# Four block products of seven multiplications per feed-forward input instead of three, and a pitch of 272 for the activations' halves

## The chip, the cores and the metric

The kernel runs on one core of a Trainium2 chip. The metric is the device time of one execution in microseconds (us). The kernel before was run three times: 2631.84, 2633.85 and 2634.01 us, median 2633.85 us. Engines are named as the profile names them: PE is the matrix engine (its weight loads are listed apart, as PEld), DVE the vector engine, ACT the scalar engine, POOL the GpSimd engine, SP the engine that issues most transfers.

## What is computed

A trunk of two layers over 256 tokens of 2048 features, all in float32. Each layer has three sublayers, and each ends in a residual sum and a layer norm:

```python
x <- LN(a*x + 0.5*SwiGLU_1(x))
x <- LN(a*x + Mixer_i(x))        # layer 0: attention, layer 1: causal pooling
x <- LN(a*x + 0.5*SwiGLU_2(x))

def swiglu(x, w_in, w_out):
    a, gate = jnp.split(x @ w_in, 2, axis=-1)
    return (jax.nn.silu(a) * gate) @ w_out
```

So there are four feed-forward blocks. In each, `w_in` is 2048 x 8192: 4096 columns for `a` and 4096 for `gate`. They are taken as eight column pairs, a pair being 512 columns of `a` and the 512 of `gate` that they are multiplied with. `w_out` is 4096 x 2048.

## The kernel before, in words

**Precision.** A float32 product is made of fp32r matmuls. Every operand is split in two: ACT rounds it into a high half (a cast to fp32r), and DVE subtracts that from the source and leaves the low half. A product is high x high + high x low + low x high, accumulated in PSUM. Activations are kept split, weights are split as they arrive. The activations of the trunk are `xs` (line 60): four tiles of 128 partitions x 4 x 2 x `W`, with `W` = 258: 256 tokens and two columns that carry the gain and the bias of the norm ahead (written by `Norm.__init__`, line 224). `xs[k][:, 0]` is the high half of block k, `xs[k][:, 1]` the low one, 258 floats (1032 bytes) further on.

**The input side of a feed-forward block** is `ffn_in`, called four times. It makes the eight column pairs in three ways:

- Pair 0 by `gemm`, feature by feature, where the norm ahead is applied meanwhile.
- Pairs 1 to 4 in plain columns: `column` (line 327) takes 128 columns of `w_in` over all 2048 rows as one transfer of 1 MB into a `raw` tile, splits it in two halves of 128 x 1024 (ACT line 324, DVE line 325), and runs for each of the 16 blocks of rows one matmul of 512 columns (line 341) and one of 256 (line 345). ACT copies the bank out (line 350), DVE adds its two halves (line 524). Two such columns, one of `a` and one of `gate`, make a feature, so a pair is eight units of this kind: every second unit ends in a silu on ACT (line 529), the others in a product on DVE (line 535). There are 32 units in each `ffn_in`.
- Pairs 5 to 7 (`SEVENS` = 3) by `Seven.run` (line 377): tokens, rows and columns are halved, and seven products of half-size blocks take the place of eight (Strassen-Winograd). For each of eight steps i it loads 1 MB of weights, splits two of the blocks as they are (512 and 1024 elements a partition), forms `ta` (1024) and `tb` (twice 512) on DVE (line 400), splits these too (1024 each), and runs seven products of three matmuls of 512 columns (lines 422 to 424). Seven PSUM banks are held by it; the eighth is for units. At its end ACT copies one bank and DVE makes seven sums of 512 (line 434), then come silu on ACT and two products of 512 on DVE (line 473), and, later, sixteen transposes of 128 columns on PE (line 481), two to a copy of ACT (line 483 has four copies). The stationary operands of its first products are `xs`; the others are `s` tiles that `Seven.prepare` makes once per `ffn_in`.

**The order around the change.** Units are emitted into the block products by `between`, a function that `Seven.run` calls after each half of a step: in the version before, after the second half of steps 0 to 6 and the first half of step 7, so eight per pair, and one more when the pair is done. Four units stand ahead of the first pair, one behind the last. After the last pair come `settle` (line 107 on ACT, line 108 on DVE: the split of the 32 gated features, as `g`) and the product with `w_out` (lines 164, 167; its weights are split at lines 140 and 141). The emitted order is the priority of each instruction; a planner that simulates the program fixes the order on each engine before the run, and moves units, settles and first splits of `w_out` where it sees an engine free. At run time each engine works in that order.

**Buffers.** Three `raw` tiles, six `whi` and six `wlo` tiles of 128 x 1024. A unit takes two of each, a step of `Seven.run` three and a half. The DVE and ACT work on weights can therefore be less than two steps ahead of PE.

**Memory.** `vecs` (line 96) holds 176 floats. The tiles of the activations, the weights and the features lie behind it. In pooling, `evac_u` (line 693) takes its `u` from a pair of buffers of its own, tag `z`.

Of the kernel before, what the change touches and what calls it, by code (L numbers as in the profile page):

```python
# [8 lines left out]
F32 = mybir.dt.float32  # L9
F32R = mybir.dt.float32r  # L10
# [3 lines left out]
P = 128  # L14
T = 256
D = 2048
KT = D // P
W = T + 2
WARM = 9
FF = 2 * D  # L20
HEADS = 8
INNER = HEADS * P
WINDOWS = (2, 4, 8, 16)

SEVENS = 3
PARTS = ('', '_columns', '_seven')
ALPHA = 4 ** 0.25
SB_SCALE = P ** -0.5
# [2 lines left out]
VECS = [  # L31
    'l0_ln1_g', 'l0_ln1_b', 'l0_ln2_g', 'l0_ln2_b', 'l0_ln3_g', 'l0_ln3_b',
    'l1_ln1_g', 'l1_ln1_b', 'l1_ln2_g', 'l1_ln2_b',
    'l1_pool_scale',
]
# [3 lines left out]
def trunk(ctx: ExitStack, tc: tile.TileContext, a: dict, out: bass.AP):  # L39
    nc = tc.nc  # L40
    const = ctx.enter_context(tc.tile_pool(name="const", bufs=1))
# [15 lines left out]
    xq = [res.tile([P, 4, T], F32, tag=f"xq{q}", name=f"xq{q}") for q in range(4)]  # L57
    xf = [x[:, j] for x in xq for j in range(4)]

    xsq = [res.tile([P, 4, 2, W], F32R, tag=f"xs{q}", name=f"xs{q}") for q in range(4)]  # L60
    xs = [x[:, j] for x in xsq for j in range(4)]
    whole = [x[:, :, :T] for x in xs]

# [29 lines left out]
                   allow_small_or_imprecise_dtypes=True)  # L93
    rcount = const.tile([P, WINDOWS[-1]], F32, name="rcount")
    nc.vector.reciprocal(rcount, count)
    vecs = const.tile([P, len(VECS) * KT], F32, name="vecs")

    def vec(name, t):
        c = VECS.index(name) * KT + t
# [113 lines left out]
    class Norm:  # L213
# [3 lines left out]
        def __init__(self, gname, bname):  # L217
            self.g, self.b = gname, bname
            self.sums = res.tile([P, 2, 2 * T], F32, tag="sums", name="sums")
            lo, hi = VECS.index(gname) * KT, VECS.index(bname) * KT  # L220
            gb = vecs[:, lo:lo + 2 * KT].rearrange("p (j t) -> p t j", j=2)
            assert hi == lo + KT
            for q in range(4):
                h, l = (xsq[q][:, :, i, T:] for i in range(2))
                nc.scalar.copy(h, gb[:, 4 * q:4 * q + 4])
                nc.vector.tensor_tensor(out=l, in0=gb[:, 4 * q:4 * q + 4], in1=h.bitcast(F32), op=ALU.subtract)

# [219 lines left out]
    def ffn_in(w_in, w_columns, w_seven, norm, hooks=None):  # L447
# [108 lines left out]
        lates = []  # L556

        def between(i, h):
            if h == 1 or i == 7:
                unit()  # L560
            if lates and (i, h) == (0, 1):
                lates.pop()()
# [121 lines left out]
    def pooling(p, norm):  # L684
# [5 lines left out]
        def evac_u(grp, nm):  # L690
            def evac(f, ps):
                win = WINDOWS[grp]
                u = tmp.tile([P, T], F32, tag="z", name="u")
                bias = total(u, ps, nm)
                if bias is not None:
                    nc.scalar.activation(u, u, AF.Identity, bias=bias)
                s, n = u, 1
                while n < win:
                    s2 = tmp.tile([P, T], F32, tag="win", name="win")
                    nc.vector.tensor_copy(s2[:, :n], s[:, :n])  # L700
                    nc.vector.tensor_tensor(out=s2[:, n:], in0=s[:, n:], in1=s[:, :T - n], op=ALU.add)
                    s, n = s2, 2 * n
                q = wide("q")[:, :T]
                nc.vector.tensor_tensor(out=q[:, :win], in0=s[:, :win], in1=rcount[:, :win], op=ALU.mult)
                nc.vector.tensor_scalar(out=q[:, win:], in0=s[:, win:], scalar1=1.0 / win, scalar2=None, op0=ALU.mult)
                nc.vector.tensor_tensor(out=q, in0=q, in1=u, op=ALU.subtract)
                split(pooled[4 * grp + f], q, q)
            return evac
# [35 lines left out]
    def last(p, norm):  # L744
        w_out = a[f'{p}ffn2_w_out']
        c = 0.5 / ALPHA
        z = [None] * 4
# [12 lines left out]

        gs = ffn_in(*(a[f'{p}ffn2_w_in' + x] for x in PARTS), norm, hooks=turn)
        for i, name in enumerate((f'{p}ln3_g', f'{p}ln3_b')):
            gb = res.tile([P, 4, 2 * W], F32, tag=f"xs{i}", name=f"gb{i}")
            for q in range(4):
                gq = gb[:, q, :512]
                nc.gpsimd.dma_start(gq, a[name][q * 512:(q + 1) * 512].partition_broadcast(P))
                gains.append(gq)
# [101 lines left out]
```

## Time and profile before

| what | value |
|---|---|
| median of three runs | 2633.85 us |
| the profiled execution, its own time | 2632.2 us |
| its span, first to last instruction | 2630.5 us |
| PE busy | 2612.0 us, 99% |
| PEld busy | 2277.8 us, 87% |
| DVE busy | 2084.0 us, 79% |
| ACT busy | 1518.1 us, 58% |
| POOL busy | 11.9 us |
| moved by DMA | 499.53 MB, mean 190 GB/s |
[...]

Busy time is the time in which an engine has at least one instruction running. Instructions of one engine overlap at their ends, so the duration of one is longer than the distance from its start to the next start; what an engine can do in a stretch is read from the starts. Matmul ends are modelled, so PE at 99% may still be slower than it could be.

### The profile page before, as it was taken

How to read it: one execution, taken by the hardware profiler on the slowest of the kernel's cores; microseconds unless marked ns; L12 is line 12 of the kernel's file. 1: busy time of each engine (PE TensorE's matmuls, PEld its weight loads, DVE VectorE, ACT ScalarE, POOL GpSimd, SP SyncE). 2: the span in 40 equal slices, each digit the busy share in tenths (PEclk: the TensorE clock that was granted, in tenths of full speed). 3: DMA queues.
4: the chain of work that ended last, by engine and by line, in shares of the span. 5: the costliest groups of instructions: out<-in, count | busy, mean ns of one | idle time of the engine just before them, and what ended most of it. 6: DMA issues, size and time to landing. Idle time of an engine off the chain costs nothing.

```text
span 2630.5 us, 37467 instructions
## 1 busy us (share of the span) xinstructions
PE 2612.0 (99%) x14828; PEld 2277.8 (87%) x14828; DVE 2084.0 (79%) x2798; ACT 1518.1 (58%) x2130; POOL 11.9 (0%) x28
## 2 busy tenths in 40 slices
PE   9999999999999999999999999999999999999998
PEld 8888888899997888888988888889888898888886
DVE  7899967585689989765799897657878799999645
ACT  6565654466576656644666566445555566656432
POOL 0000000000000000000000000000000000000000
PEclk9999999999999999999999999999999999999999
DMA  7555555554455555555455555554555545555653
GB/s 262 187 208 178 206 209 184 187 179 161 156 177 176 202 198 202 199 180 195 171 191 192 192 196 207 190 192 162 203 183 190 188 154 195 200 198 202 230 195 119
DMA packets 71519, 499.53 MB, mean 190 GB/s; under 512 B 7984, under 2 KB 8624, under 8 KB 12080
## 3 DMA queue, kind: packets, MB, share of 16 engines
q1 hardware_dynamic: 70704, 495.05, 53.7%
q8 instruction: 116, 1.90, 0.3%
q0 software_dynamic: 640, 2.10, 0.2%
q14 instruction: 59, 0.48, 0.1%
HBM read 495.02 MB, written 2.10 MB: 189 GB/s over the span
## 4 chain that ended last, share of the span: by engine, by line
PE 94%; DVE 3%; ACT 1%; issue 1%; DMA 0%; SPq 0%; DVEq 0%; ACTq 0%
PE ps L164 21%; PE pc L341 17%; PE ps L167 11%; PE pc L345 9%; PE p L422 5%; PE p L423 5%; PE p L424 5%; PE ps L159 4%; PE ps L158 4%; PE ps L160 4%; PE y L806 2%; PE y L804 2%; PE y L805 2%; DVE wlo L325 1%; PE v L660 1%
## 5 line engine op out<-in xcount | busy, mean ns | idle before, releaser
L141 DVE TENSOR_TENSOR wlo<-raw,whi 128x1024 fp32r<-128x1024 f32 (+1 forms) x498 | 595.9, 1200 | 407.7 <-ACT whi L140 407.2
L140 ACT CAST whi<-raw 128x1024 fp32r<-128x1024 f32 (+1 forms) x498 | 510.1, 1032 | 548.3 <-PE ps L164 336.6
L341 PE MATMUL pc<-xs,whi 128*128 128x512 f32 x2048 | 729.2, 396 | 1.4 <-ACT gw L483 0.7
L345 PE MATMUL pc<-xs,wlo 128*128 128x256 f32 x2048 | 554.9, 281 | 0.0
L164 PE MATMUL ps<-g,whi 128*128 128x512 f32 x1536 | 537.7, 396 | 0.0
L325 DVE TENSOR_TENSOR wlo<-raw,whi 128x1024 fp32r<-128x1024 f32 (+1 forms) x448 | 487.9, 1103 | 39.3 <-ACT whi L324 21.6
L324 ACT CAST whi<-raw 128x1024 fp32r<-128x1024 f32 (+1 forms) x448 | 417.7, 959 | 164.0 <-PE pc L341 110.8
L341 PEld LDWEIGHTS pc<-xs,whi 128*128 128x128 f32 x2048 | 385.1, 189 | 87.3 <-ACT gw L483 2.6
L167 PE MATMUL ps<-g,wlo 128*128 128x256 f32 x1536 | 427.3, 280 | 0.0
L345 PEld LDWEIGHTS pc<-xs,wlo 128*128 128x128 f32 x2048 | 386.7, 189 | 11.4
L164 PEld LDWEIGHTS ps<-g,whi 128*128 128x128 f32 x1536 | 287.1, 188 | 66.8
L167 PEld LDWEIGHTS ps<-g,wlo 128*128 128x128 f32 x1536 | 289.8, 189 | 1.5
L159 PE MATMUL ps<-xs,whi 128*128 128x258 f32 (+1 forms) x768 | 218.3, 284 | 0.0
L158 PE MATMUL ps<-xs,whi 128*128 128x258 f32 (+1 forms) x768 | 217.6, 283 | 0.0
L160 PE MATMUL ps<-xs,wlo 128*128 128x258 f32 (+1 forms) x768 | 216.5, 282 | 0.0
L164 PE MATMUL ps<-xs,whi 128*128 128x512 f32 x512 | 180.2, 398 | 0.6 <-ACT whi L140 0.6
L350 ACT COPY col<-pc 128x512 f32<-128x512 f32 x128 | 75.3, 588 | 151.6 <-PE pc L341 145.3
L422 PE MATMUL p<-whi,s 128*128 128x512 f32 x384 | 150.9, 395 | 0.9 <-ACT col L350 0.7
L423 PE MATMUL p<-whi,s 128*128 128x512 f32 x384 | 149.8, 392 | 0.0
L160 PEld LDWEIGHTS ps<-xs,wlo 128*128 128x128 f32 x768 | 146.2, 190 | 0.0
L159 PEld LDWEIGHTS ps<-xs,whi 128*128 128x128 f32 x768 | 145.4, 189 | 0.2
L158 PEld LDWEIGHTS ps<-xs,whi 128*128 128x128 f32 x768 | 144.6, 188 | 0.0
(196 smaller groups left out, 4120.9 us busy)
## 6 DMA issues: line engine op xcount, KB each, us to landing
raw<-in_l_ffn_w_in_columns SPq DMA_DIRECT2D x128, 1024.0 KB, 4.9
raw<-in_l_ffn_w_out SPq DMA_DIRECT2D x127, 1024.0 KB, 4.8
raw<-in_l_ffn_w_in_seven SPq DMA_DIRECT2D x96, 1024.0 KB, 4.9
raw<-in_l_pool_w_in SPq DMA_DIRECT2D x32, 1024.0 KB, 4.9
raw<-in_l_ffn_w_in SPq DMA_DIRECT2D x28, 1024.0 KB, 4.9
raw<-in_l_sb_w_qkv SPq DMA_DIRECT2D x24, 1024.0 KB, 4.8
raw<-in_l_pool_w_out SPq DMA_DIRECT2D x16, 1024.0 KB, 4.9
raw<-in_l_sb_w_o SPq DMA_DIRECT2D x8, 1024.0 KB, 4.9
```

The source lines that it names most:

```text
L140: nc.scalar.copy(hi[:, i], src)
L141: nc.vector.tensor_tensor(out=lo[:, i], in0=src, in1=hi[:, i].bitcast(F32), op=ALU.subtract)
L158: nc.tensor.matmul(ps[:, :one], hi[:, cs], x[:, 0, :one], start=first, stop=False)
L159: nc.tensor.matmul(ps[:, :one], hi[:, cs], x[:, 1, :one], start=False, stop=False)
L160: nc.tensor.matmul(ps[:, :one], lo[:, cs], x[:, 0, :one], start=False, stop=last)
L164: nc.tensor.matmul(ps.rearrange("p (h n) -> p h n", h=2), hi[:, cs], x, start=first, stop=last)
L167: nc.tensor.matmul(ps[:, :T], lo[:, cs], x[:, 0], start=False, stop=False)
L324: nc.scalar.copy(hi, src)
L325: nc.vector.tensor_tensor(out=lo, in0=src, in1=hi.bitcast(F32), op=ALU.subtract)
L341: nc.tensor.matmul(ps.rearrange("p (h n) -> p h n", h=2), his[k], whole[k], start=k == 0, stop=k == KT - 1)
L345: nc.tensor.matmul(ps[:, :T], los[k], whole[k][:, 0], start=False, stop=False)
L422: nc.tensor.matmul(p, xh, hi, start=i == 0, stop=False)
```

## The change

`SEVENS` goes from 3 to 4: pair 4 moves from plain columns to `Seven.run`. There are then 24 units in each `ffn_in`, four ahead of the first pair and five for each of the four pairs: after the second halves of steps 1, 3 and 5, after the first half of step 7, and when the pair is done. No unit is left for the place behind the last pair. The halves of `xs` get a pitch of 272 floats (1088 bytes); what is read of them stays the same. `vecs` gets eight unused floats, so each tile behind it starts 32 bytes later. `u` in pooling takes the buffers of tag `gate`, which the feed-forward block and the grouped product of pooling also use. The host lays out the weights by `SEVENS`, so the bytes go where the new pairs want them.

```diff
-SEVENS = 3
+PITCH = 272
+SEVENS = 4
...
-    xsq = [res.tile([P, 4, 2, W], F32R, tag=f"xs{q}", name=f"xs{q}") for q in range(4)]
+    xsq = [res.tile([P, 4, 2, PITCH], F32R, tag=f"xs{q}", name=f"xs{q}") for q in range(4)]
...
-    vecs = const.tile([P, len(VECS) * KT], F32, name="vecs")
+    vecs = const.tile([P, len(VECS) * KT + 8], F32, name="vecs")[:, :len(VECS) * KT]
...
-                h, l = (xsq[q][:, :, i, T:] for i in range(2))
+                h, l = (xsq[q][:, :, i, T:W] for i in range(2))
...
         def between(i, h):
-            if h == 1 or i == 7:
+            if (i, h) in ((1, 1), (3, 1), (5, 1), (7, 0)):
                 unit()
...
-                u = tmp.tile([P, T], F32, tag="z", name="u")
+                u = tmp.tile([P, T], F32, tag="gate", name="u")
...
-            gb = res.tile([P, 4, 2 * W], F32, tag=f"xs{i}", name=f"gb{i}")
+            gb = res.tile([P, 4, 2 * PITCH], F32, tag=f"xs{i}", name=f"gb{i}")
```

## Rows read from the trace of the kernel before

**Rows 1.** The page: busy time, share and instructions of each engine.

```profile
PE 2612.0 (99%) x14828; PEld 2277.8 (87%) x14828; DVE 2084.0 (79%) x2798; ACT 1518.1 (58%) x2130; POOL 11.9 (0%) x28
```

**Rows 2.** The page: the chain that ended last, share of the span by engine.

```profile
PE 94%; DVE 3%; ACT 1%; issue 1%; DMA 0%; SPq 0%; DVEq 0%; ACTq 0%
```

**Rows 3.** Busy time by stretch, first block product to first matmul of w_out, four blocks.

```profile
core 0: us, PE busy (x) PEld busy (x) DVE busy (x) ACT busy (x) POOL busy (x), PEclk, DMA share, GB/s
76.32:353.00 276.68, 276.39 (x1417) 233.85 (x1416) 251.91 (x309) 174.56 (x229) 0.00 (x0) 1.00 0.56 198
806.21:1086.50 280.29, 277.93 (x1418) 233.48 (x1417) 260.58 (x324) 178.76 (x237) 0.00 (x0) 1.00 0.56 197
1337.58:1616.47 278.89, 277.67 (x1420) 233.67 (x1418) 258.68 (x322) 178.21 (x236) 0.00 (x0) 1.00 0.56 197
2167.23:2444.11 276.88, 276.50 (x1421) 234.08 (x1419) 255.44 (x316) 177.15 (x237) 3.89 (x7) 1.00 0.57 200
```

**Rows 4.** The same view: the four units ahead of block two's stage.

```profile
783.70:806.21 22.51, 22.51 (x131) 19.66 (x129) 22.51 (x37) 12.27 (x18) 0.00 (x0) 1.00 0.49 169
```

**Rows 5.** Timeline of PE in block one: start, length; between the first two, 37 more.

```profile
165.66 0.40 PE L422 MATMUL p<-whi,xs 128*128 128x512 f32 x1
...
174.45 0.40 PE L341 MATMUL pc<-xs,whi 128*128 128x512 f32 x1
...
183.60 0.60 PE L481 MATMUL gt<-ident,c 128*128 128x128 f32 x4
183.96 0.48 PE L424 MATMUL p<-wlo,xs 128*128 128x512 f32 x1
...
336.15 0.39 PE L341 MATMUL pc<-xs,whi 128*128 128x512 f32 x1
...
353.00 0.38 PE L481 MATMUL gt<-ident,c 128*128 128x128 f32 x2
```

**Rows 6.** Timeline of DVE, one step of a block product and a unit's sum.

```profile
106.97 1.22 DVE L325 TENSOR_TENSOR wlo<-raw,whi 128x1024 fp32r<-128x1024 f32 x1
108.10 0.68 DVE L400 TENSOR_TENSOR tb<-raw,ta 128x512 f32<-128x512 f32 x1
108.70 1.22 DVE L325 TENSOR_TENSOR wlo<-raw,whi 128x1024 fp32r<-128x1024 f32 x1
109.84 0.68 DVE L400 TENSOR_TENSOR tb<-raw,tb 128x512 f32<-128x512 f32 x1
110.44 0.42 DVE L524 TENSOR_TENSOR col<-col 128x256 f32<-128x256 f32 x1
110.78 1.82 DVE L325 TENSOR_TENSOR wlo<-raw,whi 128x512 fp32r<-128x512 f32 x2
```

**Rows 7.** DVE's groups from 806.21 to 1086.50: busy, mean ns, idle before.

```profile
L108 DVE TENSOR_TENSOR g<-gw,g 128x256 fp32r<-128x256 f32 x25 | 9.7, 416 | 0.3 <-ACT g L107 0.3
L141 DVE TENSOR_TENSOR wlo<-raw,whi 128x1024 fp32r<-128x1024 f32 x5 | 6.0, 1209 | 0.0
```

**Rows 8.** What DVE waited for from 806.21 to 1086.50: total, times, longest.

```profile
DVE wlo L325 <- ACT whi L324: 5.3, 8, 1.8
DVE ta L400 <- DMA raw<-in_l_ffn_w_in_seven: 5.2, 6, 1.5
DVE wlo L325 <- PE pc L345: 5.1, 7, 1.6
```

**Rows 9.** The page: ACT's group of weight splits in the stages.

```profile
L324 ACT CAST whi<-raw 128x1024 fp32r<-128x1024 f32 (+1 forms) x448 | 417.7, 959 | 164.0 <-PE pc L341 110.8
```

**Rows 10.** The page: transfers of units and of block products, count, size, landing.

```profile
raw<-in_l_ffn_w_in_columns SPq DMA_DIRECT2D x128, 1024.0 KB, 4.9
raw<-in_l_ffn_w_in_seven SPq DMA_DIRECT2D x96, 1024.0 KB, 4.9
```

**Rows 11.** Timeline of PE in the last product; between the two, 40 more.

```profile
2549.65 0.39 PE L804 MATMUL y<-wlo,g 128*128 128x512 f32 x1
...
2558.94 0.39 PE L806 MATMUL y<-whi,g 128*128 128x512 f32 x1
```

**Rows 12.** Busy time of the engines in the pooling layer.

```profile
1812.00:2012.00 200.00, 200.00 (x1228) 178.77 (x1227) 165.43 (x346) 117.72 (x200) 0.00 (x0) 1.00 0.53 184
```

## The prediction

> **What bounds the kernel now.** I read the page first: PE is busy 99% of the span and DVE 79% [rows 1], and the chain of work that ended last lies on PE for 94% [rows 2]. As averages they say that PE bounds the kernel and that DVE has a fifth of the span to spare. The change touches four stretches only, so the next view is busy time by stretch, from the first block product of each `ffn_in` to the first matmul of `w_out` [rows 3]. There PE has no gap worth naming, but DVE works 1026.6 of 1112.7 us, 92%, and in the units ahead of such a stretch 22.51 of 22.51 [rows 4]. So where the change acts the reserve of DVE is 86.1 us in all four blocks, 21.5 in each, and no more. The reader is to compare what the change saves on PE with what it asks of DVE.
>
> **PE.** Three units in a row take 353.00 - 336.15 = 16.85 us, so 5.62 each; eight fewer save 44.9 us per block [rows 5]. A pair by block products is 8 x 7 x 3 = 168 matmuls; an unbroken run of 38 took 8.79 us from start to start, 231.3 ns each, so 38.9 us, and four transposes took 0.36 us, so sixteen 1.4 [rows 5]. Added: 40.3. Net 4.6 us less per block, 18.5 in all. If PE stayed the bound this would be the gain.
>
> **DVE.** Durations overlap, so I take distances from start to start: 1.135 us for 1024 elements (106.97 to 108.10, 108.70 to 109.84), 0.60 for 512, 0.34 for 256 [rows 6]. A step of a block product has four operations of 1024 (three low halves and `ta`) and three of 512 (one low half, `tb` twice): 4 x 1.135 + 3 x 0.60 = 6.34, eight steps 50.7. The end of a pair has seven sums and two products of 512: 5.4. Added: 56.1 us per block. A unit has two low halves, one sum of 256 and, every second time, one product of 256: 2 x 1.135 + 0.34 + 0.17 = 2.78; eight fewer remove 22.2. Net 33.9 us more per block, 135.6 in all. That is over the reserve of 86.1: DVE takes the bound in these stretches. Per pair with its five units DVE needs 56.1 + 13.9 = 70.0 us and PE 40.3 + 28.1 = 68.4.
>
> [...] By full durations (1.22, 0.68, 0.42) a pair costs 61.4 us, eight units 24.4, and the net is 37.0 instead of 33.9, 12.4 us more in all. The starts in the trace are 0.08 us closer than the durations, so the trace disagrees and the sum goes by starts.
>
> **What DVE can put off.** In the second block's stretch it also ran 25 settles and 5 first splits of `w_out` [rows 7]. For `w_out` to begin, four settles and one split are enough; 21 x 0.34 + 4 x 1.135 = 11.6 us can follow later, where a chunk of `w_out` needs two splits, 2.3 us of DVE, for sixteen pairs of matmuls, as many as a unit has (5.6 us of PE). I take the same for all four: 46.6. What DVE must do inside is 1026.6 + 135.6 - 46.6 = 1115.6 us.
>
> **What is lost between.** DVE waited in block two for ACT's high halves 5.3 us, for transfers 5.2, for buffers that PE freed late 5.1 [rows 8]. The last goes when PE is the one that waits, and transfers are asked for when DVE and ACT free a `raw` tile. The bounds for what remains are 0, as in the saturated stretch [rows 4], and 5.3; no row is nearer, and I take the middle, 2.65, or 10.6 in all. Behind DVE's last low half PE still has half a unit, 2.8 us (bounds 0 and 5.6): 11.2. The four stretches then take 1115.6 + 10.6 + 11.2 = 1137.4 us instead of 1112.7: 24.7 more.
>
> **ACT, transfers, order.** ACT gains 27 high halves of 1024 and 512 and the pair's copies, and loses sixteen halves of 1024, eight copies and four silus, by 0.96 us for the halves [rows 9] about 10 us per block; it is busy 178.8 of 280.3 [rows 3], so DVE hides it at no cost (without that cover up to 10 per block). Bytes are equal, eight transfers of 1024 KB for a pair either way [rows 10], and each queue issues as many. The last pair has no unit behind its own any more; its sums, silus, products and transposes are 5.4 us of DVE and some 5 of ACT and PE, and its four features come last in `w_out`, so the earlier 28 hide them: nothing, or some 5 us per block if the planner puts the transposes ahead of `w_out`. `u` shares buffers with another tile: in pooling PE is busy 200.00 of 200.00 us with DVE at 83% [rows 12], so nothing, bounds 0 and one wait of some 0.4 us for each of sixteen tiles, 6.6.
>
> **The pitch.** The only rows that bear on it are spacings of matmuls of 512 columns: 231.3 ns where every other group reads `xs`, 9.29 us / 41 = 226.6 ns where none does [rows 5, 11]. Inside the stretches a faster PE waits for DVE. Outside, `xs` is read at such widths by 512 matmuls of 512 columns (block one's first pair, pooling) and 192 of attention's values: 704 x 4.7 ns = 3.3 us less if all the difference is the pitch. I take that. The bounds are a loss as large, and a gain on every matmul outside, some 8640 x 4.7 ns = 40.6 us, since the eight extra floats move all tiles.
>
> **The sum.** 24.7 - 3.3 = 21.4 us on the profiled execution's 2632.2 (a span of 2630.5 and 1.7 around it; 1.65 under the median of the three runs): **2653.6 us**. With each bound at its kind end (no idle time, no tail, all 30 operations put off) it is 2621.7, with most at the other 2680.
>
> **The rivals.** *PE stays the bound*: faster. DVE would find room for 33.9 us per block by working ahead or putting more off, and the gain on PE shows: 2632.2 - 18.5 - 3.3 = 2610.4. It decides where DVE's work inside falls below 272 us per block, with 260.6 + 33.9 = 294.5 in block two. For it: the planner moves settles and splits freely. Against it: only 14 us of such work is there, six buffers hold less than two steps, and ahead of the stretch DVE has no gap [rows 3, 4, 7].
> *The end of each pair*: slower still. If the sums stand in DVE's order ahead of the next pair's splits, DVE waits for PE's last products and PE then for banks. At each of 16 ends half of the 5.4 us would be lost on top: 43 us, 2696.8. For it: with one unit less ahead of them, covers are shorter. Against it: DVE's waits today name no bank.
> *Addresses matter everywhere*: faster. If the pitch and the shift of 32 bytes bring all matmuls outside the stretches to the better spacing, it is 2653.6 - 40.6 + 3.3 = 2616.3. Against it: features and weights have even pitches already, and the spacing of 226.6 ns was reached with the old start. [...]
> *The units do not stay where they are put*: three ran back to back before `w_out` [rows 5], though they are emitted apart. That moves PE's work and leaves DVE's sum, so it is the forecast's time.
>
> **How the numbers follow.** The forecast, with the last point, has 0.62; PE as the bound 0.13, the ends of pairs 0.15, addresses 0.10. 0.2% is 5.3 us, about what a measurement of this kernel can tell from no change. PE as the bound and the addresses are faster, 0.23, of which 0.02 may end within the bound. Of the forecast's 0.62 some 0.11 lie within it, at its kind end. So faster 0.21, the same 0.13, and slower 0.66, which is the rest of the forecast and the ends of pairs. The range of 2612 to 2684 takes in the forecast's own, 2622 to 2680, and the rival of the addresses; it leaves out about half of the first rival and most of the second.
>
> **What would show it.** Right: in the four stretches DVE busy 97% or more, PE 3 to 5% idle, its gaps ended by DVE's low halves (line 325), stretches of 280 to 290 us; settles moved behind the start of `w_out`. Wrong: PE without gaps in stretches of 272 us (first rival); DVE idle at pair ends with sums as the late ones (second); a spacing under 226 ns in the last product (third). I would also be wrong if DVE's distances from start to start changed with the new addresses, which no row excludes.

## The result, and the profile after

The changed kernel takes 2703.69 us (median of 4 runs, 2701.59 to 2705.42), the kernel before beside it 2633.93 us: ratio 1.0266, 95% interval 1.0253 to 1.0279. It is slower, as forecast, but by 70 us where 20 were forecast, and above the stated range of 2612 to 2684. Line numbers after the change are two higher than before.

The page: busy time, share and instructions of each engine, and the chain that ended last.

```profile
PE 2624.9 (97%) x14508; PEld 2263.7 (84%) x14508; DVE 2210.3 (82%) x2946; ACT 1549.7 (57%) x2166; POOL 11.9 (0%) x28
...
PE 73%; DVE 20%; issue 5%; ACT 2%; DMA 0%; SPq 0%; DVEq 0%; ACTq 0%
```

Against [rows 1, 2], DVE's share of the chain went from 3% to 20%. The busy shares of the whole span hardly tell it. The four stretches do (busy time by stretch, first block product to first matmul of `w_out`, then the sum):

```profile
79.44:370.23 290.79, 277.30 (x1340) 228.91 (x1338) 284.47 (x346) 184.13 (x240) 0.00 (x0) 0.98 0.54 191
824.74:1122.94 298.20, 280.88 (x1340) 229.44 (x1338) 293.09 (x362) 187.71 (x248) 0.00 (x0) 0.97 0.54 188
1374.67:1668.33 293.66, 276.66 (x1340) 225.90 (x1338) 291.15 (x360) 186.91 (x247) 0.00 (x0) 0.99 0.54 189
2221.15:2515.57 294.42, 279.86 (x1341) 229.96 (x1339) 286.74 (x353) 186.92 (x248) 4.49 (x8) 0.97 0.55 191
sum 1177.07, PE 1114.70 PEld 914.20 DVE 1155.45 ACT 745.67 POOL 4.49; mean PE 278.68 PEld 228.55 DVE 288.86 ACT 186.42 POOL 1.12
```

They grew from 1112.7 [rows 3] to 1177.1 us, 64.3 of the 73.2 by which the spans differ (2703.7 and 2630.5). (Block one's stretch in [rows 3] ends at two transposes ahead of `w_out`; to the first matmul of `w_out` itself the four are 1112.9 us, as in the tables below.) DVE is busy 98% of them. What it did not put off, its groups in block two's stretch:

```profile
L110 DVE TENSOR_TENSOR g<-gw,g 128x256 fp32r<-128x256 f32 x24 | 8.6, 414 | 0.0
L143 DVE TENSOR_TENSOR wlo<-raw,whi 128x1024 fp32r<-128x1024 f32 x6 | 7.2, 1215 | 0.0
```

24 settles and 6 splits of `w_out`, where before there were 25 and 5 [rows 7]; the other three blocks have the same counts. Its waits in the same stretch, 4.9 us in all, where before there were three of over 5 us [rows 8]:

```profile
DVE wlo L327 <- ACT whi L326: 4.2, 4, 1.5
DVE col L526 <- ACT col L352: 0.7, 2, 0.5
```

**Where PE loses time.** A product's matmul is listed as 0.40 us long and starts 0.23 us behind the one before it (161.07 to 161.30), so PE's busy time hides small losses. So I sum over all matmuls of the stretches the distance from start to next start, less what it is unhindered: 231 ns for a product, 235 and 120 ns for a unit's matmuls of 512 and 256 columns, 90 for a transpose. What is over is called lost; what is left is PE's own work. A loss counts for the step of the product that follows it. The places: the first pair; behind the ends of pairs (steps one to five of the pairs behind the first); the last pair from step six on; the end (behind the last product). A rest of at most 4 us is not shown, and a number below zero means matmuls a little closer than these distances. Times in us, over all four stretches:

| kernel | stretches | DVE busy | PE's own work | lost | first pair | pairs' ends | last pair | end |
|---|---|---|---|---|---|---|---|---|
| before | 1112.9 | 1026.8 | 1108.3 | 4.6 | 3.3 | 3.8 | -0.7 | -0.9 |
| after | 1177.1 | 1155.5 | 1084.7 | 92.4 | 7.1 | 45.2 | 19.4 | 22.0 |

The change saved PE 23.6 us of its own work, and lost 87.8. Three places carry nearly all of that. A few rows from each in block one:

*Behind a pair's end*, PE's timeline, a transpose of the pair before, then a product of the next:

```profile
154.26 0.27 PE L483 MATMUL gt<-ident,c 128*128 128x128 f32 x1
156.48 0.50 PE L424 MATMUL p<-whi,s 128*128 128x512 f32 x1 [1.95 <-ACT whi L326]
```

DVE meanwhile:

```profile
152.80 0.68 DVE L402 TENSOR_TENSOR tb<-raw,ta 128x512 f32<-128x512 f32 x1
153.41 0.68 DVE L436 TENSOR_TENSOR c<-p,su 128x512 f32<-128x512 f32 x1
154.01 0.41 DVE L526 TENSOR_TENSOR col<-col 128x256 f32<-128x256 f32 x1
154.34 0.68 DVE L402 TENSOR_TENSOR tb<-raw,tb 128x512 f32<-128x512 f32 x1
```

ACT's row for the high half that PE waits for:

```profile
155.38 1.04 ACT L326 CAST whi<-tb 128x1024 fp32r<-128x1024 f32 x1 [0.33 <-DVE tb L402]
```

PE waits for a high half that ACT makes of `tb`, and DVE finishes `tb` at 155.02 only, because a sum of the pair before and a unit's sum stand between the halves of `tb`. DVE is without a pause; it is late.

*In the last pair*, settles stand inside the steps (DVE's timeline; between these two rows ten more settles). PE waits for a low half that stands behind twelve of them, and then for the high half of a `tb` that DVE finishes behind all fourteen (PE's timeline):

```profile
321.49 0.74 DVE L110 TENSOR_TENSOR g<-gw,g 128x256 fp32r<-128x256 f32 x2
...
332.73 0.74 DVE L110 TENSOR_TENSOR g<-gw,g 128x256 fp32r<-128x256 f32 x2
```

```profile
332.86 0.73 PE L426 MATMUL p<-wlo,s 128*128 128x512 f32 x2 [0.67 <-DVE wlo L327]
335.21 0.79 PE L424 MATMUL p<-whi,s 128*128 128x512 f32 x1 [1.62 <-ACT whi L326]
```

*At the end*, PE's timeline from the last unit's last matmul to `w_out`:

```profile
364.27 0.39 PE L343 MATMUL pc<-xs,whi 128*128 128x512 f32 x1
369.88 0.69 PE L483 MATMUL gt<-ident,c 128*128 128x128 f32 x2 [5.22 <-DVE c L475]
370.22 0.78 PE L166 MATMUL ps<-g,whi 128*128 128x512 f32 x1
```

DVE does splits of `w_out` and settles ahead of the product that the transposes wait for:

```profile
364.40 1.21 DVE L143 TENSOR_TENSOR wlo<-raw,whi 128x1024 fp32r<-128x1024 f32 x1
365.53 0.41 DVE L526 TENSOR_TENSOR col<-col 128x256 f32<-128x256 f32 x1
365.87 1.22 DVE L143 TENSOR_TENSOR wlo<-raw,whi 128x1024 fp32r<-128x1024 f32 x1
367.00 1.08 DVE L110 TENSOR_TENSOR g<-gw,g 128x256 fp32r<-128x256 f32 x3
368.01 1.21 DVE L143 TENSOR_TENSOR wlo<-raw,whi 128x1024 fp32r<-128x1024 f32 x1
369.14 0.68 DVE L475 TENSOR_TENSOR c<-c,c 128x512 f32<-128x512 f32 x1
```

Behind such a wait `w_out` starts slowly (busy time in its first 8 us, the clock is the third number from the end):

```profile
370.23:378.30 8.07, 8.07 (x36) 7.01 (x35) 5.13 (x9) 3.01 (x6) 0.00 (x0) 0.65 0.51 183
```

36 matmuls at a mean granted clock of 0.65: 0.50 from 370.23 to 375.83, 1.00 from there to 378.30. The clock falls inside the stretches too, where before it was 1.00 throughout [rows 3]. In block one it falls three times, each time during or shortly behind a wait of PE of 1.6 to 2.0 us; this stretch follows the wait at a pair's end shown above:

```profile
157.40:160.70 3.30, 3.30 (x11) 2.29 (x10) 3.30 (x5) 3.30 (x5) 0.00 (x0) 0.50 0.52 221
```

At a granted clock of 0.50 a product's matmul starts 0.43 us behind the one before it (159.10 to 159.53), at 1.00 0.23. In the four stretches the granted clock is 0.50 for 41 us ahead of the ends. So by estimate, 41 x (1 - 0.23 / 0.43), some 19 of the 92.4 us lost are slower matmuls and not waits.

### The profile page after: what moved, and what is told of

It reads as the page before. It is cut to its first block, busy times and chain, and to the rows that moved or that the text cites. A ratio compares the mean times of both kernels' runs of the same rounds, so it can differ in the third digit from the quotient of the medians.

```text
span 2703.7 us, 37135 instructions
## 1 busy us (share of the span) xinstructions
PE 2624.9 (97%) x14508; PEld 2263.7 (84%) x14508; DVE 2210.3 (82%) x2946; ACT 1549.7 (57%) x2166; POOL 11.9 (0%) x28
## 4 chain that ended last, share of the span: by engine, by line
PE 73%; DVE 20%; issue 5%; ACT 2%; DMA 0%; SPq 0%; DVEq 0%; ACTq 0%
PE ps L166 20%; PE ps L169 10%; DVE wlo L327 9%; PE pc L343 6%; PE p L424 4%; PE p L425 4%; PE p L426 4%; PE ps L160 4%; PE ps L162 4%; PE ps L161 4%; PE pc L347 3%; PE y L806 2%; PE y L808 2%; PE y L807 2%; DVE tb L402 2%
## 5 line engine op out<-in xcount | busy, mean ns | idle before, releaser
L143 DVE TENSOR_TENSOR wlo<-raw,whi 128x1024 fp32r<-128x1024 f32 (+1 forms) x498 | 595.7, 1201 | 409.4 <-ACT whi L142 408.6
L142 ACT CAST whi<-raw 128x1024 fp32r<-128x1024 f32 (+1 forms) x498 | 509.8, 1032 | 536.3 <-PE ps L166 336.0
L343 PE MATMUL pc<-xs,whi 128*128 128x512 f32 x1536 | 542.2, 394 | 0.0
L327 DVE TENSOR_TENSOR wlo<-raw,whi 128x512 fp32r<-128x512 f32 (+1 forms) x448 | 466.2, 1062 | 0.6 <-ACT whi L326 0.5
L326 ACT CAST whi<-raw 128x512 fp32r<-128x512 f32 (+1 forms) x448 | 393.3, 924 | 42.0 <-PE pc L343 25.4
L347 PE MATMUL pc<-xs,wlo 128*128 128x256 f32 x1536 | 415.6, 281 | 0.5 <-DVE wlo L327 0.4
L326 ACT CAST whi<-tb 128x1024 fp32r<-128x1024 f32 x128 | 134.6, 1052 | 133.3 <-DVE tb L402 128.3
L426 PE MATMUL p<-wlo,s 128*128 128x512 f32 x512 | 183.6, 403 | 7.6 <-DVE wlo L327 7.6
L327 DVE TENSOR_TENSOR wlo<-tb,whi 128x1024 fp32r<-128x1024 f32 x128 | 155.9, 1218 | 15.5 <-ACT whi L326 14.6
L326 ACT CAST whi<-ta 128x1024 fp32r<-128x1024 f32 x128 | 134.3, 1049 | 58.4 <-DVE ta L402 53.4
```

Of the source, the lines that this page charges most:

```text
L142: nc.scalar.copy(hi[:, i], src)
L143: nc.vector.tensor_tensor(out=lo[:, i], in0=src, in1=hi[:, i].bitcast(F32), op=ALU.subtract)
L326: nc.scalar.copy(hi, src)
L327: nc.vector.tensor_tensor(out=lo, in0=src, in1=hi.bitcast(F32), op=ALU.subtract)
L343: nc.tensor.matmul(ps.rearrange("p (h n) -> p h n", h=2), his[k], whole[k], start=k == 0, stop=k == KT - 1)
L347: nc.tensor.matmul(ps[:, :T], los[k], whole[k][:, 0], start=False, stop=False)
```

## The experiments

All ratios are against the kernel before, run beside. The expectations call the steps of a block product chunks. Diffs are against the changed kernel unless another base is named.

### The parts alone

e1: the pitch, the shift and the new tag of `u`, with three pairs.

```diff
-SEVENS = 4
+SEVENS = 3
...
-            if (i, h) in ((1, 1), (3, 1), (5, 1), (7, 0)):
+            if h == 1 or i == 7:
```

> Theory W (DVE's work): the loss of 70 us is DVE's load in the four stretches of block products, and what PE waits for behind it; the pitch has no part in it. With three block products again and the pitch, the eight floats and the buffers of u as changed, the time is that of the kernel before less what PE's spacing gains: 2620 to 2634 us, DVE busy some 1025 us in the four stretches. Rival A (addresses): the new addresses cost time themselves, by slower matmuls or by the low clock of the first 20 us; then 2645 us or more.

2628.31 us (11 runs), 0.9979 [0.9970, 0.9988]: a gain of 0.2%. The stretches:

```profile
sum 1107.68, PE 1103.30 PEld 933.09 DVE 1026.94 ACT 708.39 POOL 3.84; mean PE 275.83 PEld 233.27 DVE 256.74 ACT 177.10 POOL 0.96
```

The gain lies inside the stretches (1112.9 to 1107.7), where PE bounds: there the median distance of a unit's matmuls is 232 and 117 ns, where before it was 235 and 119. The pitch, the shift and the tag were not run apart.

e2: the fourth pair with the old pitch, `vecs` and tag (base: the kernel before).

```diff
-SEVENS = 3
+SEVENS = 4
...
-            if h == 1 or i == 7:
+            if (i, h) in ((1, 1), (3, 1), (5, 1), (7, 0)):
```

> Four block products with the old pitch, the old vecs and u in its own buffers. Theory W: the whole loss is here, 2700 to 2712 us. Rival A: most of it is gone, 2634 to 2660.

2701.54 us, 1.0257 [1.0243, 1.0271]. The fourth pair, with the places of the units that go with it, is the whole loss. Both times lie where theory W had them. With four pairs the pitch brings nothing (2701.54 without, 2703.69 with); that a faster PE only waits for DVE there, busy 1155.1 of 1175.1 us, is the likely reason.

### Much less work for DVE

e3: no low halves of `tb`.

```diff
-                ht, lt = pair()
-                parts(ht, lt, tb)
+                ht = whis.tile([P, 2, 512], F32R, tag="whi", name="whi")
+                lt = la
+                nc.scalar.copy(ht, tb)
```

> The changed kernel without the low halves of tb: products 6 and 4 take those of ta in their place, so the matmuls are as many, the result is another one, and DVE has 32 operations of 1024 less per block, 36 us, 145 in all. Theory W: DVE's work in the stretches falls to some 1010 us, below PE's 1090, and PE is the bound: 2605 to 2630 us. Rival O (order at pair ends: the sums, silus and banks make PE wait, whatever DVE has to do): 2670 to 2700, since the sums stand where they were.

2615.07 us, 0.9931 [0.9917, 0.9944], in theory W's range. The stretches:

```profile
sum 1093.51, PE 1079.59 PEld 905.97 DVE 1021.64 ACT 753.92 POOL 4.49; mean PE 269.90 PEld 226.49 DVE 255.41 ACT 188.48 POOL 1.12
```

With DVE's work at 1021.6 us PE's own 1084.7 is what counts, and the stretches are shorter than with three pairs. So DVE's work is what makes the change slow. One thing goes with it: each step also takes one buffer for low halves less, and e3 does not tell what that alone is worth; but e5 and e13 below take work from DVE without freeing a buffer, and gain too.

### The end of the stretch

e4: the last pair's transposes and last four settles behind `w_out`'s fifth chunk.

```diff
-        lates.pop()()
...
-        settle(range(16, 32))
-        return gs
+        settle(range(16, 28))
+
+        def rest():
+            lates.pop()()
+            settle(range(28, 32))
+        return gs, rest
...
```

> The changed kernel with the transposes of the last pair and the last four settles emitted behind the fifth chunk of w_out instead of ahead of w_out. Theory W: PE no longer waits 5.2 us ahead of w_out for the last pair's products, which stand in DVE's order behind settles and splits of w_out, and the clock does not fall there: 4 x 7 to 8 us less, 2670 to 2680 us. If the wait only moves (DVE is behind anyway and w_out waits for its own splits), 2695 to 2704.

2671.37 us, 1.0141 [1.0125, 1.0156], in theory W's range: 32 us of the 70. The start of `w_out`, and the stretches:

```profile
361.73:367.80 6.07, 6.07 (x37) 5.32 (x36) 6.07 (x9) 3.12 (x5) 0.00 (x0) 1.00 0.70 255
```

```profile
sum 1155.16, PE 1112.26 PEld 912.23 DVE 1133.71 ACT 738.27 POOL 3.69; mean PE 278.06 PEld 228.06 DVE 283.43 ACT 184.57 POOL 0.92
```

The stretches are 21.9 us shorter: the loss at the end is gone (22.0 to -0.8), the other places lose as before. And `w_out` starts at a granted clock of 1.00: from its first matmul to its 37th it takes 6.26 us in block one instead of 8.52, and in the four blocks 6.8 us less. Another 3.4 us lie ahead of the first stretch. As `w_out` starts earlier, 2 or 3 of its splits and 21 or 22 settles are left in each stretch, where there were 6 and 24.

e9: a unit kept for the place behind the last pair.

```diff
-        for _ in range(4):
+        for _ in range(3):
             unit()
```

> Edit: three instead of four units ahead of the first pair, so that one of the 24 lies behind the last pair, where its matmuls cover VectorE's last products. Theory E (the wait of 5.2 us ahead of the last transposes and the half clock behind it cost some 8 us per block, the step that was priced at nothing): most of it goes, 2672 to 2685. Rival N (VectorE's work is the time also there, so the unit only moves): 2698 to 2706.

2681.44 us, 1.0185 [1.0168, 1.0202]: one unit as cover, taken from the four ahead, takes 22 us of the loss. The loss at the end is gone here too (22.0 to -1.5). Both runs show the missing cover behind the last pair as a cost.

### Less work in the units

e5: the unit's two halves added in PE's accumulation.

```diff
-                nc.tensor.matmul(ps.rearrange("p (h n) -> p h n", h=2), his[k], whole[k], start=k == 0,
-                                 stop=k == KT - 1)
+                nc.tensor.matmul(ps[:, :T], his[k], whole[k][:, 0], start=k == 0, stop=False)
+                nc.tensor.matmul(ps[:, :T], his[k], whole[k][:, 1], start=False, stop=k == KT - 1)
...
-                nc.vector.tensor_tensor(out=c[:, :T], in0=c[:, :T], in1=c[:, T:], op=ALU.add)
```

> Edit: the changed kernel, but a plain column adds its low-activation half in PE's own accumulation (a third matmul of 256 instead of half of one of 512), so VectorE's sum per unit goes. Theory W (in the stretches VectorE's own work is the time: it is 98% busy there): 24 sums of 0.335 us less per block, 32 us in all; at most a part of PE's added matmul time counts, as PE has 13 us of gaps per block: 2671 to 2682. Rival P (PE bounds, its gaps at the pairs' ends are the loss, and VectorE's busy time only follows from it): PE gets some 16 x 13 ns more per unit, 5 us per block, so 2704 to 2725.

2693.75 us, 1.0230 [1.0214, 1.0245]: neither theory. The stretches:

```profile
sum 1166.84, PE 1113.33 PEld 966.55 DVE 1127.84 ACT 728.92 POOL 4.49; mean PE 278.33 PEld 241.64 DVE 281.96 ACT 182.23 POOL 1.12
```

DVE works 27.6 us less and the stretches are 10.2 shorter: its pauses grow from 21.6 to 39.0, while PE's own work is only 6.4 more. That DVE is busy 98% does not make each microsecond of its work one of the time.

e6: the diffs of e4 and e5 together.

> Edit: the sum on PE as in the run before, and the late end together (the last pair's transposes and last four settles behind the fifth chunk of w_out). Theory W: both gains stand side by side, as one is VectorE's work and the other a wait of PE at the stretch's end: 2671 less some 25 to 32: 2639 to 2650. Rival P: 2671 or more. If PE becomes the bound in between, some 2650 to 2660.

2664.09 us, 1.0120 [1.0105, 1.0135]: in none of the expected ranges, and the same as in e5 again: 7 us below e4 for 26.6 us of DVE's work.

e11: e6 with the units behind other steps.

```diff
-            if (i, h) in ((1, 1), (3, 1), (5, 1), (7, 0)):
+            if (i, h) in ((0, 1), (2, 1), (5, 1), (7, 0)):
```

> Edit: the late end and the sum on PE, as in the run at 2664, with the units of a pair behind chunks one, three, six and the first half of chunk eight, instead of two, four, six and eight: the same work in all, but a unit covers the second chunk, where PE waits longest. Theory S: no change, 2660 to 2668. Theory L: PE's 42 us of waits in the second and third chunks shrink by a third or more: 2638 to 2655; none of it comes back in another place unless VectorE is without a pause there.

2662.19 us, 1.0109 [1.0094, 1.0124]: 2 us less than e6, within the spread. In the second and third steps of all pairs the loss fell from 42.5 to 17.1 us, more than theory L asked for, but most of it came back in other steps, the fourth and fifth above all (-1.5 to 12.5) and the sixth to eighth (13.3 to 21.1). So theory L's time failed, and the time is that of theory S.

e8: e4, with a unit's sum and product on GpSimd.

```diff
-                nc.vector.tensor_tensor(out=c[:, :T], in0=c[:, :T], in1=c[:, T:], op=ALU.add)
+                nc.gpsimd.tensor_tensor(out=c[:, :T], in0=c[:, :T], in1=c[:, T:], op=ALU.add)
...
-                nc.vector.tensor_tensor(out=pair[:, t % 2 * T:(t % 2 + 1) * T], in0=g, in1=s, op=ALU.mult)
+                nc.gpsimd.tensor_tensor(out=pair[:, t % 2 * T:(t % 2 + 1) * T], in0=g, in1=s, op=ALU.mult)
```

> Edit: the late end, and a unit's sum and product go from VectorE to GpSimd. Theory W: VectorE loses 24 x 0.335 + 12 x 0.34 = 12 us per block, 48 in all, and PE's own work (1113 us in the four stretches) is next: 2625 to 2645. Rival C (the two engines hold each other up when both work on the same memory): VectorE's operations get longer while GpSimd works, and the time stays at 2660 to 2690. Which it is shows in the mean duration of VectorE's splits.

2699.93 us, 1.0255 [1.0240, 1.0271], 28.6 above e4. Groups of DVE in block one's stretch, e4 and then e8, and POOL's in e8:

```profile
L327 DVE TENSOR_TENSOR wlo<-tb,whi 128x1024 fp32r<-128x1024 f32 x31 | 37.9, 1221 | 3.3 <-ACT whi L326 3.1
L402 DVE TENSOR_TENSOR tb<-raw,ta 128x512 f32<-128x512 f32 x30 | 20.6, 685 | 0.0
```

```profile
L327 DVE TENSOR_TENSOR wlo<-tb,whi 128x1024 fp32r<-128x1024 f32 x31 | 39.4, 1271 | 5.9 <-ACT whi L326 5.7
L402 DVE TENSOR_TENSOR tb<-raw,ta 128x512 f32<-128x512 f32 x30 | 23.0, 767 | 0.1
...
L526 POOL TENSOR_TENSOR col<-col 128x256 f32<-128x256 f32 x20 | 39.2, 1958 | 240.0 <-ACT col L352 205.3 <-DVE tb L402 34.7
```

Rival C held, and beyond its range: these operations of DVE are 4 and 12% longer, and a sum of 256 that took DVE 0.42 us takes POOL 1.96 on average. Over the four stretches DVE is busy 1136.8 us, against 1133.7 in e4, though some 43 us of its operations went to POOL, and its pauses grow from 21.5 to 46.1. The trace shows which operations are longer: in block one the low halves and `ta`, `tb` that overlap no operation of POOL are as long as in e4 (1.22 to 1.23 us for 1024 elements from 201.69 to 208.06, while POOL does nothing), and of those that overlap one some take 1.76 us instead of 1.22. That it is the memory on which they meet, as rival C has it, no run shows.

### Work put off by hand

e10: e4, with 24 more settles written behind `w_out`'s chunks (base: e4).

```diff
-        settle(range(8))
+        settle(range(4))
...
+        def rest(c):
+            def go():
+                if c == 4:
+                    lates.pop()()
+                settle(range(4 * c + 4, 4 * c + 8))
+            return go
+        return gs, {c: rest(c) for c in range(7)}
...
```

> Edit: the late end, and 24 more settles put off behind w_out's chunks (four behind each of the chunks one to seven), so that only four lie in the stretch. It does by hand what the prediction took VectorE to do of itself. Theory S (what counts is VectorE's work in the whole stretch): some 17 settles of 0.34 us fewer per block, 23 us in all, against the late end alone: 2645 to 2652. Theory L (what counts is where VectorE is late: the first chunks behind each pair's end; at the stretch's end the late end alone has left no wait of PE): 2668 to 2674.

2670.37 us, 1.0142 [1.0125, 1.0159], as e4. But it decides nothing between the theories: the planner drew the settles forward again. Block two's stretch, e4 and then e10:

```profile
L110 DVE TENSOR_TENSOR g<-gw,g 128x256 fp32r<-128x256 f32 x21 | 7.7, 423 | 0.0
L110 DVE TENSOR_TENSOR g<-gw,g 128x256 fp32r<-128x256 f32 x21 | 7.7, 417 | 0.0
```

e13: the same (base: e10), with each group of settles tied behind its chunk's split on ScalarE.

```diff
+    split_ins = [None]
...
-                nc.scalar.copy(hi[:, i], src)
+                split_ins[0] = nc.scalar.copy(hi[:, i], src)
...
-                settle(range(4 * c + 4, 4 * c + 8))
+                with tc.issue_after(split_ins[0].inst if hasattr(split_ins[0], "inst") else split_ins[0].ins):
+                    settle(range(4 * c + 4, 4 * c + 8))
```

> Edit: as the run at 2670 that wrote 24 settles behind w_out's chunks, but now each group of four is tied behind the split of its chunk on ScalarE, since the planner had drawn them forward again and 21 lay in the stretch as before. Theory S (VectorE's work in the whole stretch counts, so work put off to w_out is time won): up to 17 settles of 0.34 us per block, 23 us in all: 2645 to 2655. Theory L (only VectorE's lateness behind the pairs' ends counts): 2666 to 2674, with PE's lost time behind the pairs' ends as it was.

2656.28 us, 1.0091 [1.0076, 1.0106], 15 below e4. In block two's stretch four settles are left:

```profile
L110 DVE TENSOR_TENSOR g<-gw,g 128x256 fp32r<-128x256 f32 x4 | 1.5, 425 | 0.0
```

The settles that left are 17, 17, 18 and 13 in the four blocks, 65 x 0.34 = 22 us of DVE's work. The loss behind the pairs' ends is nearly as it was (45.2 and 43.3); the one of the last pair, from step six on, went from 20.7 to 2.0 us. So theory L is wrong, and S asked for a little more: put-off work is time won, about two thirds of it here, and it had cost just where the settles stood. (In three blocks `w_out` now starts ahead of the last unit's last 31 matmuls, so these stretches do not hold the same work as the others'.)

### Where relief counts

e14, e15 and e16: e4 without the low halves of `tb` in two of the eight steps.

```diff
-                ht, lt = pair()
-                parts(ht, lt, tb)
+                if i in (1, 2):
+                    ht = whis.tile([P, 2, 512], F32R, tag="whi", name="whi")
+                    lt = la
+                    nc.scalar.copy(ht, tb)
+                else:
+                    ht, lt = pair()
+                    parts(ht, lt, tb)
```

e15 has `(5, 6)` and e16 `(0, 7)` for `(1, 2)`.

> Edit: the late end (2671), and the low halves of tb left out in the second and third chunk of each pair; there products 6 and 4 take ta's low halves. It takes 32 splits of 1.135 us, 36 us, from VectorE in the chunks where PE waits. Theory S: 2632 to 2642. Theory L: the same or nearly, 2632 to 2645, with the lost time at the second and third chunk gone from 53 us to under 20.

> Edit: the same as the run before, but in the sixth and seventh chunk: VectorE has the same 36 us less to do, behind the chunks where PE waits in a pair and ahead of the pair's end. Theory S: 2632 to 2642, as there. Theory L: VectorE can't run ahead by more than its six buffers, so under half of it comes through: 2652 to 2668, and its pauses grow instead.

> Edit: the late end (2671), and the low halves of tb left out in the first and the eighth chunk of each pair, around the pair's end: the same 36 us of VectorE's work as in the two runs before (2662 in chunks two and three, 2658 in six and seven). Theory L (VectorE's work between the last products of a pair and the second chunk's tb sets PE's wait): the most of the three, 2638 to 2650, with PE's lost time in the second chunk down from 40 us to 25 or less. Rival S' (the place doesn't matter, any relief of VectorE gives about a third of itself): 2656 to 2663.

2661.73 us (1.0109 [1.0092, 1.0125]), 2657.82 (1.0097 [1.0082, 1.0113]) and 2659.71 (1.0101 [1.0084, 1.0117]). Each leaves out 36 us of DVE's splits, and they gave 10, 14 and 12 us: about a third, wherever it was left out. That is less than both theories wanted of e14; e15 came out as theory L had it, e16 as rival S'. In the stretches DVE is busy 35.8, 26.3 and 33.9 us less than in e4: in e15 the planner moved 8 us of other work in (five splits of `w_out`, three settles, four sums of units). The stretches of e14, e15 and e16:

```profile
sum 1142.76, PE 1101.84 PEld 907.10 DVE 1097.88 ACT 740.70 POOL 3.70; mean PE 275.46 PEld 226.78 DVE 274.47 ACT 185.18 POOL 0.93
```

```profile
sum 1141.14, PE 1105.98 PEld 911.32 DVE 1107.40 ACT 739.50 POOL 3.70; mean PE 276.49 PEld 227.83 DVE 276.85 ACT 184.87 POOL 0.92
```

```profile
sum 1141.64, PE 1106.48 PEld 903.49 DVE 1099.84 ACT 735.52 POOL 3.70; mean PE 276.62 PEld 225.87 DVE 274.96 ACT 183.88 POOL 0.93
```

In e14 the second and third steps of all pairs lose as much as in e4 (53.1 and 53.2 us), though it is there that splits are left out. In e16 most of the loss in the second steps is gone (40.5 to 5.0 us), and the third steps lose more (12.7 to 30.5): half of it only moved. As in e3, a buffer goes free with each split that is left out.

e17: e4 with one buffer less.

```diff
-    whis = ctx.enter_context(tc.tile_pool(name="whis", bufs=6))
-    wlos = ctx.enter_context(tc.tile_pool(name="wlos", bufs=6))
+    whis = ctx.enter_context(tc.tile_pool(name="whis", bufs=5))
+    wlos = ctx.enter_context(tc.tile_pool(name="wlos", bufs=5))
```

> Edit: the late end (2671) with five instead of six buffers for the high and for the low halves; no work changes. Theory L (the lead that VectorE can gain in the middle of a pair is bounded by these buffers, and is what carries PE over the pair's end): the lost time grows, 2680 to 2710. Rival S' (the split of VectorE's sum alone): 2668 to 2676.

2687.49 us, 1.0206 [1.0191, 1.0222], 16 above e4 and in theory L's range, with no work changed: the lead that the buffers allow is worth time. The stretches are 1168.1 us and the loss 84.1, against 1155.2 and 71.2 of e4. Seven buffers were not tried.

### All together

e18: the diffs of e4, e5, e11, e10 and e13 in one.

> Edit: four pairs with all the edits that keep the result: the late end, the settles tied behind w_out's chunks, the units' sums on PE and the units moved (2662 without the ties; the ties alone were worth 15). Theory A (the losses lie in different places: the last pair's chunks, the pairs' ends, the stretch's end): 2642 to 2650. Theory B (one shortage of VectorE moves from place to place, so the gains share it): 2651 to 2660. In neither does it come under the kernel before.

2646.02 us, 1.0050 [1.0033, 1.0067], in theory A's range: the gains add. In its stretches the clock does not fall at all; what share that has in the gain is not shown. It is the best of four pairs that keep the result, and still slower than three. What beats both kernels, by 0.2%, is e1, the new pitch with three pairs.

### What the runs give together

| kernel | stretches | DVE busy | PE's own work | over the larger |
|---|---|---|---|---|
| before | 1112.9 | 1026.8 | 1108.3 | 4.6 |
| e1, pitch alone | 1107.7 | 1026.9 | 1108.3 | -0.6 |
| e3, less work for DVE | 1093.5 | 1021.6 | 1084.7 | 8.8 |
| e18, all | 1122.2 | 1096.0 | 1090.4 | 26.2 |
| e14, relief | 1142.8 | 1097.9 | 1084.0 | 44.9 |
| e16, relief | 1141.6 | 1099.8 | 1084.0 | 41.8 |
| e6, late end, sum on PE | 1145.0 | 1107.1 | 1090.4 | 37.9 |
| e11, e6 with units moved | 1140.2 | 1108.0 | 1090.4 | 32.2 |
| e15, relief | 1141.1 | 1107.4 | 1084.0 | 33.7 |
| e5, sum on PE | 1166.8 | 1127.8 | 1091.1 | 39.0 |
| e10, put off by order | 1150.1 | 1131.1 | 1084.0 | 19.0 |
| e4, late end | 1155.2 | 1133.7 | 1084.0 | 21.5 |
| e8, sum on POOL | 1182.9 | 1136.8 | 1084.0 | 46.1 |
| e17, five buffers | 1168.1 | 1139.6 | 1084.0 | 28.5 |
| e2, four alone | 1175.1 | 1155.1 | 1084.7 | 20.0 |
| after | 1177.1 | 1155.5 | 1084.7 | 21.6 |

The rows stand by how far DVE's work lies above PE's (e9 and e13 are left out, as their stretches do not hold the same work). A stretch is not as long as the larger of the two works. Where PE's is the larger, by 63 to 82 us, the two hide one another but for 9 us at most. Where DVE's is the larger by up to 37 us, 26 to 45 are added, the 26 in e18, where few settles stand in the way and the clock does not fall; where it is the larger by 47 to 71, 19 to 29 (e8, where DVE's operations are longer beside POOL's, 46). So at an equal distance a full DVE cost more than a full PE in these runs. What relief takes from DVE comes back in large part as its own pauses (21.5 us in e4, 33.7 to 44.9 in e14 to e16), which is why it gave a third. That the buffers are part of the reason e17 shows; how the rest divides between them, ACT's order, the clock and the ends of pairs stays open.

## Why the prediction was wrong

Right: the side, the mechanism (DVE takes the bound in the four stretches, 98% busy), and of these terms the first two, roughly, the sum in the third, and the fourth.

- *PE, -18.5 us*: its own work, counted at the fixed distances above, fell by 23.6. The prediction, and the text ahead of it, count sixteen transposes for a pair and two to a copy; the trace before has 96 transposes and 24 copies of them for twelve pairs, so eight and four to a copy. With eight the term is -21.4.
- *DVE, 135.6 us more*: 128.7 measured (1155.5 - 1026.8). The sum by starts held, by durations it would have been 148.
- *What is lost between and the tail, 10.6 + 11.2*: DVE's pauses are 21.6 us. The sum of the two came out right by luck; its parts are wrong, as DVE has no pause at the end.
- *ACT, about 10 us per block, hidden*: 9.2 (745.7 against 708.7 us in the stretches), though a pair gains 24 high halves of 1024 and eight of 512, not 27 in all.
- *The pitch, -3.3 outside*: not so. With three pairs the new pitch, with the shift and the tag, gains 5 us inside the stretches and nothing outside; with four pairs it gains nothing. Why addresses should matter to PE, no run shows; nothing of the 40 us came.

**The step that failed is "What DVE can put off", 46.6 us.** Nothing was put off: 24 settles and 6 splits stand in every stretch, against 25 and 5 before. The prediction took the planner's freedom as freedom to move work behind; it moved settles forward, into the last pair's steps, where DVE was late already, and even when they were written behind `w_out`'s chunks (e10). With 46.6 added back to 1137.4 and DVE's work at its measured value, 6.7 less than the predicted 1162.2, the stretches come to 1177.3; 1177.1 was measured. That it fits to 0.2 us is luck in part, as said of the pauses. e13 is the counterpart: there the late end and the ties do put the work off, to 4 settles and 2 splits in three blocks (8 and 3 in the fourth), and the kernel takes 2656.28 us where 2653.6 were forecast. But not every microsecond put off came through: tied behind, settles worth 22 us gave 15, and relief in other places a third.

**The second miss is the price of "nothing" for the last pair without a unit behind it.** Its other end, some 5 us per block if the transposes come ahead of `w_out`, is what happened: PE stands 5.2 us in blocks one, two and four and 5.8 in block three, and the clock is 0.65 to 0.76 in the first 8 us of `w_out`. e4 measures both: 21.9 us in the stretches and 6.8 behind them. The two misses overlap: what DVE does during this wait is the work that was not put off (three or four splits of `w_out` and two or three settles per block leave the stretch with e4), so the 21.9 are not to be added to the 46.6. The clock was not in the sum at all: behind the four starts of `w_out` 60 matmuls take 8.0 us more than before, most of the 8.9 by which the rest of the span grew (73.2 - 64.3; another 3.1 lie ahead of the first stretch, and some 2 are won elsewhere), and in the stretches, by the estimate above, some 19 of the 92.4 us lost go with it.

Of the rivals, *the end of each pair* named the place and, by luck, nearly the price, 43 us at sixteen ends; 45.2 are lost behind twelve. Its mechanism is not what the trace shows: DVE's waits in the stretches of blocks one and two name ACT alone, never PE's last products; it has too much to do. *PE stays the bound* would have needed DVE near e3's 1021.6 us.

What I said would show it: DVE over 97% came; PE is idle 5.3% by its busy time (1114.7 of 1177.1) and loses 7.8% by distances, where I said 3 to 5; the stretches are 291 to 298 us where I said 280 to 290; no settles moved behind the start of `w_out`; PE's gaps in block one are ended by ACT's high halves more than by DVE's low ones (weight loads that waited):

```profile
PEld p L424 <- ACT whi L326: 9.3, 10, 2.1
PEld gt L483 <- DVE c L475: 5.5, 1, 5.5
PEld p L426 <- DVE wlo L327: 2.6, 4, 1.1
```

ACT is only the last link: it waits for `tb`, as its row behind the pair's end shows.

## What to carry to other kernels

A change that takes work from the bound engine and gives more to one that is nearly full makes two engines of nearly equal work. Here the stretch was then longer than the larger of the two, with DVE as the larger by 19 to 45 us in some 1150, and mostly by more where the two works were closer. Don't count relief of the fuller engine at more than a part. Work that could follow later did so here only when its order was tied: look where the planner put such work before the change, and take it to be there after. And ask of each stage's end what covers its last dependent steps; a wait there was paid twice, as the clock fell with it.

## What the runs showed of the hardware

- Behind a wait of PE of 5.2 us (369.88) the granted clock was 0.50 from 370.23 to 375.83: the first 36 distances of `w_out` took 8.52 us instead of the 6.26 of e4, which has no such wait. Inside the changed kernel's stretches it also fell during or behind waits of 1.6 to 2.0 us (0.50 from 157.40 to 160.70, where a product's matmul starts 0.43 us behind the one before, instead of 0.23); in e18 it did not fall at all.
- With three pairs, the pitch of 1088 instead of 1032 bytes for the halves of `xs`, the shift of 32 bytes and the new tag of `u` together gained 0.2% of the time; with four pairs nothing (2703.69 us with them, 2701.54 without).
- A sum of 256 elements took POOL 1.96 us on average in block one of e8 where DVE took 0.42, and two kinds of DVE's own operations were 4 and 12% longer there (1271 ns instead of 1221, 767 instead of 685); those that overlapped no operation of POOL were not (1.22 to 1.23 us for 1024 elements from 201.69 to 208.06).
